# A chunked scan beside two projections: the diagonal part with 64-column sums of squares moved apart from the off-diagonal and state's part

## The chip, the cores and the metric

The kernel runs on one core of a Trainium2 chip. The metric is the device time of one execution in microseconds. The core's engines work side by side and wait for each other by semaphores: PE (TensorE) does matrix products, DVE (VectorE), ACT (ScalarE) and POOL (GpSimd) do elementwise work, SP issues DMAs. Each engine takes its own instructions in the order in which the kernel wrote them.

## What is computed

The reference is a trunk of two layers on a sequence of 1024 tokens of width 1024, in float32. Layer 0 is a spatial gating mixer; layer 1, which the change touches, is a Mamba-2 SSD mixer with 32 heads of 64 channels in 8 groups and a state of 128:

```python
def ssd_mixer(h, w_in, conv_w, conv_b, dt_bias, a_log, d_skip, norm_w, w_out):
    proj = h @ w_in
    z = proj[..., :D_INNER]
    xbc = jax.nn.silu(causal_depthwise_conv(xbc, conv_w, conv_b))
    ...
    w_ls = (cb[..., None] * decay * dt[:, :, None])
    y_diag = jnp.einsum('bclsgj,bcsgjp->bclgjp', w_ls, x)
    states = jnp.einsum('bclgn,bclgj,bclgjp->bcgjpn', Bm, decay_to_end * dt, x)
    _, prev = lax.scan(step, init, (states, chunk_decay))
    y_off = jnp.einsum('bclgn,bcgjpn,bclgj->bclgjp', Cm, prev, jnp.exp(dA_cs))
    y = y_diag + y_off + x * d_skip
    gated = (y * jax.nn.silu(z)).reshape(bsz, L, B_GROUPS, D_INNER // B_GROUPS)
    gated = rmsnorm(gated, norm_w)
    return gated @ w_out
```

Within each chunk of 128 tokens every token sees the earlier ones of its chunk directly (the diagonal part), and all before the chunk through a state that is carried from chunk to chunk (the off-diagonal part). The group norm at the end needs, for each token, the sum of the squares of a group's 256 channels.

## The kernel before

The last third of the kernel is the scan. Its main loop (`scans`) goes over 8 groups x 8 chunks; n = 8·group + chunk counts them. Beside the scan PE works through projections that are still due (`fill`: those of four groups, later the output product), so that it always has something to do. The order on every engine is written out by hand: the loop calls one small function after the other, and `project(upto)` lets the projections catch up to a mark that `want` works out. One step of a projection is six matmuls of 512 columns.

Each chunk calls, on PE:

- `pe_b(n)`: four diagonal matmuls into the tile `yy` (L1626; heads in pairs, 64 columns of the array each, so that two of them lie side by side), two off-diagonal matmuls into the other half of `yy` (L1630, they read the state of chunk n-1), one matmul that makes the state's input `sp` (L1637). In every fourth chunk, with `ends`, two or four matmuls with a column of ones follow, which sum the squares of half a sequence of an earlier group into the other half of `sp` (`sum_b`, L1702), and ACT copies two rows of the result out (L1706). In float32 each of these matmuls is two instructions on PE.
- `project(want(n + .5))`, the first half chunk of projections.
- `pe_a(n + 2)`: three transposes and the B-C product of the chunk after next into `tp` (L1593, L1594).
- `project(want(n + 1))`, the second half.

Behind `pe_a`, and in this order, DVE does `weights(n+1)` (L1617: the decay times the B-C product, which the next diagonal reads), `update(n)` (L1656: state from `sp`), `out(n)` (L1668: off-diagonal part times decay; L1671: both parts and the skip together), one operation of `drain()`, as a rule a tap of the convolution on a finished accumulator `ab` of the projections (L1322), then `tokens(n+2)` (L1607, L1609, from `tp`). ACT makes the decays (L1599, L1601), copies from `tp` (L1611), squares (L1689), casts weights for the projections (L111) and applies silu (L1433, L1423). POOL adds the two output parts (L1674), carries the state (L1647), scales tokens (L1612), gates (L1678), adds the squares' two halves ahead of the sums (L1696) and splits weights (L112).

`yy`, `sp`, `tp` and `pr` (the sums after the scan) share four PSUM tiles of one bank each; an engine that touches a tile waits for the one that used the same bank before. Projections have two accumulators `ab`: the one after next takes over the first one's tile once its last tap is done.

Of the kernel before, what the change touches and what calls it, by code (L numbers as in the profile page):

```python
# [22 lines left out]
G = 8  # L23
# [6 lines left out]
def kernel(  # L30
# [21 lines left out]
    nc = tc.nc  # L52
    x = x[0]
    out = out[0]
# [42 lines left out]
    def sm(name):  # L97
        return ps[0].tile([P, 512], F32, name=name, tag="sm", bufs=n_sm[0])
# [65 lines left out]
    ones = cst.tile([P, P], F32, name="ones")  # L164
# [1146 lines left out]
    def convolve():  # L1311

        finish()
        if todo:
            late.append(todo.pop(0)())
# [75 lines left out]
    def drain(n=1):  # L1391

        for _ in range(min(n, len(queue))):
            for f in queue.pop(0):
                f()
# [153 lines left out]
    def prefetch(g, th):  # L1549

        st = sts[g]
        if g in xbc_d:
            t = st["xbc", th] = s8([P, 4, 512], "xbc")
            nc.sync.dma_start(out=t, in_=xbc_d[g][:, th])
        ze = st["ze", th] = s8([P, 4, 512], "ze")
        if g < G - 1:
            nc.sync.dma_start(out=ze[:, 0:2], in_=z_d[g][:, :, th * 512:(th + 1) * 512])
        for f in range(2):
            for pt in range(2):
                h = 4 * g + 2 * pt + f  # L1560
                nc.sync.dma_start(out=ze[f * 64:(f + 1) * 64, 2 + pt],
                                  in_=ecs_d[h, th * 512:(th + 1) * 512].partition_broadcast(64))

    class Scan:
# [55 lines left out]
        def pe_b(self, c, ends=None):  # L1620

            w, wl = self.cw[c], self.wl.pop(c)
            yy = sm("yy")
            for j in range(4):
                pt, f = j // 2, j % 2
                nc.tensor.matmul(out=yy[f * 64:(f + 1) * 64, pt * P:(pt + 1) * P], lhsT=w[:, j * 64:(j + 1) * 64],  # L1626
                                 rhs=wl[:, j, :], start=True, stop=True)
            if c > 0:
                for pt in range(2):
                    nc.tensor.matmul(out=yy[:, 256 + pt * P:384 + pt * P],  # L1630
                                     lhsT=self.state[c - 1][:, pt * P:(pt + 1) * P], rhs=self.x(3, c),
                                     start=True, stop=True)
            sp = None
            if c < 7 or ends is not None:
                sp = sm("sp")
            if c < 7:
                nc.tensor.matmul(out=sp[:, 0:256], lhsT=w[:, 512:640], rhs=w[:, 256:512], start=True, stop=True)  # L1637
            if ends is not None:
                ends.sum_b(sp[:, 256:512], 2 if ends.g == G - 1 else 1)
            self.ps[c] = yy, sp  # L1640

        def carry(self, c):

# [54 lines left out]
        def sum_b(self, pr=None, n=1):  # L1698
            pr = sm("pr") if pr is None else pr
            for m in range(n):  # L1700
                for h in range(2):
                    nc.tensor.matmul(out=pr[h * 64:h * 64 + 1, 0:256], lhsT=ones[:, 0:1],  # L1702
                                     rhs=self.sq[:, m, h * 256:(h + 1) * 256], start=m == 0, stop=m == n - 1)
            self.sr = self.sq[:, 1, 0:256]
            for h in range(2):
                nc.scalar.copy(out=self.sr[h * 64:h * 64 + 1], in_=pr[h * 64:h * 64 + 1, 0:256])  # L1706
# [5 lines left out]
    def group_rstd(g, t0, n):  # L1712


        c = n // P
        sv = tiny([P, 8], "sv")[:, 0:c]
        nc.sync.dma_start(out=sv, in_=ss_d[g, t0:t0 + n].rearrange("(p c) -> p c", c=c))
        got = []

        def guess():  # L1720
            nc.vector.tensor_scalar(sv, sv, 1.0 / 256, NORM_EPS, ALU.mult, ALU.add)
            got.append(rsqrt_a(sv, c))

        def tail():
            rv = tiny([P, 8], "rvv")[:, 0:c]
            rsqrt_b(rv, sv, got[0], c)
            got.append(rv)

        def put():
            nc.sync.dma_start(out=rs_d[g, t0:t0 + n].rearrange("(p c) -> p c", c=c), in_=got[1])  # L1730

        return guess, tail, put
# [117 lines left out]
    def scans():  # L1850


        chunks = [(g, c) for g in range(G) for c in range(8)]
        N, M = len(chunks), 50
        scan, rs, ran = {}, {}, [0]
        total = 32 * len(plain)

        def fill():
            yield from pj
            yield from bo.product(1, hook_b)  # L1860

        fl = fill()

        def project(upto):
            while ran[0] < upto:
                next(fl, None)
                ran[0] += 1

        def want(at):
            if at < M:  # L1870
                return AHEAD + (total - AHEAD) * at // M
            return total + min(16 * (at - M) // (N - 5 - M), 16 + 2 * (at - N + 5))

        def at(f, n, *a):
            if 0 <= n < N:
                g, c = chunks[n]
                if g not in scan:
                    scan[g] = Scan(g, nc.gpsimd)
                getattr(scan[g], f)(c, *a)

        prefetch(0, 0)
        project(AHEAD // 2 + 1)
        while todo or late:
            convolve()
        for n in range(2):
            at("load", n)
        drain(1)
        for n in range(2):
            at("decay", n)
        drain(len(queue))  # L1890
        at("pe_a", 0), at("tokens", 0), at("weights", 0)
        drain(len(queue))
        project(AHEAD)
        at("pe_a", 1), at("tokens", 1), at("weights", 1)
        at("load", 2)
        for n, (g, c) in enumerate(chunks):
            if n == M + 3:
                drain(len(queue))
            elif n == N - 9:
                for k in range(2):  # L1900
                    bo.get("a", 0, 0, k)
            elif n == N - 7:
                end["scan"] = scan[G - 1]
                bo.get("b", 0, 0, 0)
            p = g if c >= 4 else g - 1
            at("pe_b", n, scan[p] if c % 4 == 3 and p >= 0 else None)
            project(want(n + .5))
            at("pe_a", n + 2)
            if n > 0:
                at("weights", n + 1)  # L1910
            at("update", n)
            at("out", n)
            at("decay", n + 2)
            at("carry", n + 1)
            drain()
            at("tokens", n + 2)
            at("gate", n)
            if n >= N - 7:
                k = n - N + 7
                if k % 2:  # L1920
                    bo.prep(1, k // 2)
                else:
                    bo.ready(0, 0, k // 2)
            at("load", n + 3)
            th = 0 if c >= 4 else 1
            if p >= 0:
                sc = scan[p]
                if p == G - 1:
                    if c == 5:
                        sc.gate_half(th), sc.squares(th)  # L1930
                elif c % 4 == 0:
                    sc.squares(th)
                elif c % 4 == 1:
                    sc.store(th)
                    sc.sum_a()
            if c % 4 == 0 and n >= 8:
                scan[g - 1].sum_c(1 - th)
            if g > 0:
                if c == 5:
                    rs[g] = group_rstd(g - 1, 0, T)  # L1940
                elif c == 6:
                    rs[g][0]()
                elif c == 7:
                    rs[g][1]()
            if c == 0 and g > 1:
                rs[g - 1][2]()
            if c == 1:
                prefetch(g, 1)
            if c == 5 and g < G - 1:
                prefetch(g + 1, 0)  # L1950
            project(want(n + 1))
        sc = scan[G - 1]
        for k in (0, 1):
            bo.get("a", 0, 1, k)
        bo.get("b", 1, 0, 0)
        sc.sum_c(0), rs[G - 1][2]()
        bo.prep(1, 3)
        sc.gate_half(1), sc.squares(1)
        end["half"] = [group_rstd(G - 1, 0, 512)]
        for k in (0, 1):  # L1960
            bo.get("a", 1, 0, k)
        while ran[0] < total + 31:
            project(ran[0] + 1)
        sc.sum_b(n=2)
        sc.sum_c(1)
        for _ in fl:
            pass
# [22 lines left out]
    with tc.manual_schedule():  # L1990
        scans()
        into_end()
# [28 lines left out]
```

## Time and profile before

| What | us |
|---|---|
| median of 3 runs (lowest, highest) | 1517.45 (1517.34, 1518.26) |
| the profiled execution, its own time | 1520.45 |
| its span from the first to the last instruction | 1518.6 |
| busy in the span: DVE, ACT, POOL | 1052.2, 783.3, 402.8 |
| the scan's 64 chunks, first diagonal to last | 1021.7 to 1355.7 of the span |
| PE busy in those 334.0 us | 330.8 |
| DVE, ACT, POOL busy in them | 244.5, 228.1, 222.7 |

Rows of a timeline read: start in us of the span, duration in us, engine, line, operation, output <- inputs, shape, how many were merged; in brackets the idle time of the engine ahead of it and what ended that. Matmuls overlap, so what counts on PE is the distance between starts. Rows of waits read: total us, times, longest.

### The profile page before, as it was taken

What the parts mean: (1) busy time and instruction counts of PE and PEld (TensorE: products, weight loads), DVE (VectorE), ACT (ScalarE), POOL (GpSimd) and SP (SyncE); (2) the same over time, 40 slices, a digit from 0 to 9 for tenths busy, and PEclk for the clock granted to TensorE, in tenths of its full rate; (3) what the DMA queues carried; (4) which work ended last, traced back from release to release, by engine and by line L of the source; (5) the groups of instructions that cost most, each with busy time, mean ns of one, the idle gap of its engine ahead of it and who ended that gap; (6) DMA issues with size and microseconds to landing.
All of it is one profiled execution on the core that took longest, in us unless ns stands there. A gap on an engine that the chain in (4) does not pass through costs nothing. (4 is left out here: it accounts for less than half of the span.)

```text
span 1518.6 us, 21307 instructions
## 1 busy us (share of the span) xinstructions
PE 1475.8 (97%) x7834; PEld 1219.9 (80%) x7834; DVE 1052.2 (69%) x1713; ACT 783.3 (52%) x1256; POOL 402.8 (27%) x451
## 2 busy tenths in 40 slices
PE   6899999999999999999999999989999999999997
PEld 6899988888888888877878788877777777777875
DVE  7956566676666655678656467867677777688876
ACT  6433332322322445556566556656676666756463
POOL 1111110000000023202131323117677666643121
PEclk9999999999999999999999999999999999999999
DMA  5554323332322999947377978787656564679973
GB/s 183 140 173 140 105 89 111 108 107 98 116 86 79 357 255 241 250 140 159 104 178 159 189 162 165 149 231 203 187 165 170 160 191 137 171 248 277 257 149 111
DMA packets 174952, 254.45 MB, mean 168 GB/s; under 512 B 16400, under 2 KB 103168, under 8 KB 171648
## 3 DMA queue, kind: packets, MB, share of 16 engines
q1 hardware_dynamic: 124768, 168.93, 36.6%
q0 software_dynamic: 42448, 70.27, 23.0%
q10 hardware_dynamic: 7632, 13.90, 2.6%
q8 instruction: 62, 1.02, 0.3%
q14 instruction: 42, 0.34, 0.1%
HBM read 186.14 MB, written 51.18 MB: 156 GB/s over the span
## 5 line engine op out<-in xcount | busy, mean ns | idle before, releaser
L134 PE MATMUL acc<-hh,wh 128*128 128x512 f32 x868 | 339.9, 392 | 1.7 <-ACT u L296 1.4
L136 PE MATMUL acc<-hh,wl 128*128 128x512 f32 x868 | 338.5, 390 | 2.0 <-DVE wl L112 1.8
L135 PE MATMUL acc<-hl,wh 128*128 128x512 f32 x868 | 337.8, 389 | 0.0
L112 DVE TENSOR_TENSOR wl<-wr,wh 128x1024 fp32r<-128x1024 f32 (+1 forms) x96 | 114.3, 1192 | 119.4 <-ACT wh L111 119.3
L136 PEld LDWEIGHTS acc<-hh,wl 128*128 128x128 f32 x868 | 162.9, 188 | 37.8 <-DVE wl L112 3.7
L134 PEld LDWEIGHTS acc<-hh,wh 128*128 128x128 f32 x868 | 163.1, 188 | 36.1 <-ACT u L296 2.3
L135 PEld LDWEIGHTS acc<-hl,wh 128*128 128x128 f32 x868 | 163.0, 188 | 33.1
L296 ACT COPY u<-acc 128x512 f32<-128x512 f32 x115 | 66.9, 583 | 197.7 <-PE acc L136 197.6
L111 ACT CAST wh<-wr 128x1024 fp32r<-128x1024 f32 (+1 forms) x112 | 115.2, 1029 | 95.4 <-PE acc L135 56.7
L136 PE MATMUL acc<-wh,hl 128*128 128x256 f32 x448 | 128.6, 287 | 4.8 <-DVE hl L407 3.4
L134 PE MATMUL acc<-wh,hh 128*128 128x256 f32 x448 | 129.2, 288 | 3.0 <-ACT hh L398 1.1
L134 PE MATMUL ab<-hh,wh 128*128 128x512 f32 x288 | 128.2, 445 | 2.8 <-DVE zt L999 1.7
L135 PE MATMUL acc<-wl,hh 128*128 128x256 f32 x448 | 128.1, 286 | 1.1 <-DVE wl L421 1.1
L136 PE MATMUL ab<-hh,wl 128*128 128x512 f32 x288 | 113.4, 394 | 0.0
L135 PE MATMUL ab<-hl,wh 128*128 128x512 f32 x288 | 112.5, 390 | 0.1
L136 PEld LDWEIGHTS acc<-wh,hl 128*128 128x128 f32 x448 | 87.1, 194 | 5.9 <-DVE hl L407 4.1
L134 PEld LDWEIGHTS acc<-wh,hh 128*128 128x128 f32 x448 | 87.3, 195 | 3.9 <-ACT hh L398 1.3
L135 PEld LDWEIGHTS acc<-wl,hh 128*128 128x128 f32 x448 | 87.2, 195 | 1.6 <-DVE wl L421 1.4
L1599 ACT ACTIVATE wl<-wl,tk 128x128 f32<-128x128 f32 x256 | 81.6, 391 | 2.2 <-DMA wl<-cs_d 1.9
L649 POOL DMA_DIRECT2D y_d<-y x8 | 4.4, 549 | 291.3 <-DVE y L646 291.3
L135 PE MATMUL bo<-wl,xh 128*128 128x512 f32 x192 | 76.2, 397 | 3.5 <-DVE wl L742 1.8
L112 DVE TENSOR_TENSOR wl<-t,wh 128x1024 fp32r<-128x1024 f32 (+1 forms) x38 | 45.5, 1196 | 48.5 <-ACT wh L111 48.4
(317 smaller groups left out, 3255.1 us busy)
## 6 DMA issues: line engine op xcount, KB each, us to landing
wr<-in_a_w_in_dram SPq DMA_DIRECT2D x48, 512.0 KB, 3.7
wl<-cs_d SPq DMA_DIRECT2D x64, 256.0 KB, 3.4
wr<-in_b_w_in_dram SPq DMA_DIRECT2D x30, 512.0 KB, 9.1
wb<-in_a_w_out_dram SPq DMA_DIRECT2D x10, 1024.0 KB, 11.8
wb<-in_b_w_out_dram SPq DMA_DIRECT2D x10, 1024.0 KB, 11.1
wr<-in_b_w_in_dram SPq DMA_DIRECT2D x36, 256.0 KB, 8.0
v<-v_d SPq DMA_DIRECT2D x8, 1024.0 KB, 4.8
y_d<-y POOLq DMA_DIRECT2D x8, 1024.0 KB, 5.8
```

Of the source, the lines that this page charges most:

```text
L111: nc.scalar.copy(out=hi, in_=src)
L112: return (eng or nc.vector).tensor_tensor(out=lo, in0=src, in1=hi.bitcast(F32), op=ALU.subtract)
L134: nc.tensor.matmul(out=o, lhsT=l[0], rhs=r[0], start=start, stop=False, **kw)
L135: nc.tensor.matmul(out=o, lhsT=l[0], rhs=r[1], start=False, stop=False, **kw)
L136: nc.tensor.matmul(out=o, lhsT=l[1], rhs=r[0], start=False, stop=stop, **kw)
L296: nc.scalar.copy(out=self.u[n][:, i], in_=a)
L649: store = lambda: nc.gpsimd.dma_start(out=y_d[-1], in_=y)
L1599: nc.scalar.activation(wl[:, j, :], wl[:, j, :], AF.Relu, scale=-1.0, bias=tokc(2, c, self.g)[:, j:j + 1])
```

## The change

`pe_b` keeps the diagonal matmuls and the sums alone. The off-diagonal matmuls and the state's input become a function of their own, `pe_c`, which is called behind the first half of the projections and ahead of the transposes of `pe_a`. `sp` is still allotted in `pe_b`. The sums now use 64 columns of ones and fill 64 rows for each half instead of one; ACT still copies one row of each.

```diff
             yy = sm("yy")
+            sp = None
+            if c < 7 or ends is not None:
+                sp = sm("sp")
             for j in range(4):
...
+            if ends is not None:
+                ends.sum_b(sp[:, 256:512], 2 if ends.g == G - 1 else 1)
+            self.ps[c] = yy, sp
+
+        def pe_c(self, c):
+            w, (yy, sp) = self.cw[c], self.ps[c]
             if c > 0:
                 for pt in range(2):
                     nc.tensor.matmul(out=yy[:, 256 + pt * P:384 + pt * P],
                                      lhsT=self.state[c - 1][:, pt * P:(pt + 1) * P], rhs=self.x(3, c),
                                      start=True, stop=True)
-            sp = None
-            if c < 7 or ends is not None:
-                sp = sm("sp")
             if c < 7:
                 nc.tensor.matmul(out=sp[:, 0:256], lhsT=w[:, 512:640], rhs=w[:, 256:512], start=True, stop=True)
-            if ends is not None:
-                ends.sum_b(sp[:, 256:512], 2 if ends.g == G - 1 else 1)
-            self.ps[c] = yy, sp
...
-                    nc.tensor.matmul(out=pr[h * 64:h * 64 + 1, 0:256], lhsT=ones[:, 0:1],
+                    nc.tensor.matmul(out=pr[h * 64:h * 64 + 64, 0:256], lhsT=ones[:, 0:64],
...
             project(want(n + .5))
+            at("pe_c", n)
             at("pe_a", n + 2)
```

On PE, in a chunk without sums (group 1, chunk 1), the order before was this, with the semaphores that a matmul waits for (PE's names for tiles: `yy`, `sp`, `ab`, `tp` as above):

```order
L1626 MATMUL yy<-wl,cw 64x128 [waits DMAHW3_49,DVE_49,Activation_49]
L1626 MATMUL yy<-wl,cw 64x128 x3
L1630 MATMUL yy<-xbc,state 128x128 [waits DVE_49]
L1630 MATMUL yy<-xbc,state 128x128
L1637 MATMUL sp<-cw 128x256 [waits Pool_49]
L134 MATMUL ab<-hh,wh 128x512
```

The same place in the changed program:

```order
L1629 MATMUL yy<-wl,cw 64x128 [waits DMAHW3_49,DVE_49,Activation_49]
L1629 MATMUL yy<-wl,cw 64x128 x3
L134 MATMUL ab<-hh,wh 128x512
L135 MATMUL ab<-hl,wh 128x512
L136 MATMUL ab<-hh,wl 128x512
L134 MATMUL ab<-hh,wh 128x512
L135 MATMUL ab<-hl,wh 128x512
L136 MATMUL ab<-hh,wl 128x512
L1639 MATMUL yy<-xbc,state 128x128 [waits DVE_49]
L1639 MATMUL yy<-xbc,state 128x128
L1643 MATMUL sp<-cw 128x256 [waits Pool_49]
```

Six projection matmuls have come between the diagonal part and the off-diagonal and state's part.

On PE, in a chunk with sums (group 1, chunk 3, n = 11), one piece of the difference:

```order
-L1626 MATMUL yy<-wl,cw 64x128 [waits DMAHW3_49,DVE_49,Activation_49]
-L1626 MATMUL yy<-wl,cw 64x128 x3
-L1630 MATMUL yy<-xbc,state 128x128 [waits DVE_49]
-L1630 MATMUL yy<-xbc,state 128x128
-L1637 MATMUL sp<-cw 128x256 [waits Pool_49]
-L1702 MATMUL sp<-gsq,ones 1x256 [waits Pool_49]
-L1702 MATMUL sp<-gsq,ones 1x256
+L1629 MATMUL yy<-wl,cw 64x128 [waits DMAHW3_49,DVE_49,Activation_49]
+L1629 MATMUL yy<-wl,cw 64x128 x3
+L1705 MATMUL sp<-gsq,ones 64x256 [waits DVE_49,Pool_49]
+L1705 MATMUL sp<-gsq,ones 64x256
 L134 MATMUL ab<-hh,wh 128x512 [waits DVE_49]
```

and the piece that follows it, half a chunk later:

```order
 L136 MATMUL ab<-hh,wl 128x512
+L1639 MATMUL yy<-xbc,state 128x128 x2
+L1643 MATMUL sp<-cw 128x256 [waits Activation_49]
 L1593 MATMUL tp<-ident,xbc 128x128 [waits PE_49]
 L1593 MATMUL tp<-ident,xbc 128x128 x2
```

The sums stand directly behind the diagonal part and wait for DVE as well as for POOL; the state's input stands behind the sums in the same tile and waits for ACT.

On DVE the order is the same in both programs. Around one chunk it reads, with the changed program's line numbers (L1659, L1671 and L1674 are L1656, L1668 and L1671 of before):

```order
L1617 TENSOR_TENSOR wl<-wl,cw 128x512 [waits DMAHW3_49,DVE_49,Activation_49]
L1659 TENSOR_TENSOR state<-sp,state 128x256 [waits PE_49,Pool_49]
L1671 TENSOR_TENSOR t_8910<-yy,ze 128x256
L1674 SCALAR_TENSOR_TENSOR cw<-xbc,dsk,yy 128x128 x2
L1322 SCALAR_TENSOR_TENSOR bc<-ab,par,bc 128x1021
L1607 TENSOR_TENSOR cw<-tp,tk 128x256 [waits DMAHW4_49,PE_49]
```

Nothing moved here; the state update, the output, the tap and the tokens stand behind each other, and the first of them waits for `sp` from PE.

## The prediction

> **What bounds the kernel now.** I began with the page's table of busy time, then the waits of PE within the scan (1017 to 1380 us of the span), then PE's timeline around single chunks, then the DVE, ACT and POOL rows that feed those chunks. Chunks are numbered n = 8·group + chunk, 0 to 63.
>
> ```profile
> span 1518.6 us, 21307 instructions
> ...
> PE 1475.8 (97%) x7834; PEld 1219.9 (80%) x7834; DVE 1052.2 (69%) x1713; ACT 783.3 (52%) x1256; POOL 402.8 (27%) x451
> ```
>
> The next two rows are the longest waits of PE's matmuls in the scan (total, times, longest).
>
> ```profile
> PE ab L134 <- DVE x L1322: 1.1, 2, 0.7
> PE yy L1626 <- DVE wl L1617: 0.7, 1, 0.7
> ```
>
> PE is the bound, and in the scan it waits for almost nothing. So the change can win only by making PE's own work shorter, and anything that now arrives just in time for PE can cost. The timeline of PE shows a chunk without sums (n = 18) and the next, with sums (n = 19):
>
> ```profile
> 1117.09 0.40 PE L136 MATMUL ab<-hh,wl 128*128 128x512 f32 x1
> 1117.42 0.66 PE L1626 MATMUL yy<-wl,cw 128*64 128x128 f32 x8
> 1118.01 0.71 PE L1630 MATMUL yy<-bc,state 128*128 128x128 f32 x4
> 1118.55 0.60 PE L1637 MATMUL sp<-cw 128*128 128x256 f32 x2
> ...
> 1119.22 0.39 PE L135 MATMUL ab<-hl,wh 128*128 128x512 f32 x1
> ...
> 1120.38 0.38 PE L1593 MATMUL tp<-ident,x 128*128 128x128 f32 x2
> 1120.59 0.27 PE L1593 MATMUL tp<-ident,bc 128*128 128x128 f32 x1
> ...
> 1122.08 0.39 PE L136 MATMUL ab<-hh,wl 128*128 128x512 f32 x1
> 1122.39 0.66 PE L1626 MATMUL yy<-wl,cw 128*64 128x128 f32 x8
> ...
> 1124.06 0.60 PE L1702 MATMUL sp<-gsq,ones 128*1 128x256 f32 x4
> 1124.59 0.50 PE L134 MATMUL ab<-hh,wh 128*128 128x512 f32 x1
> 1124.92 0.39 PE L135 MATMUL ab<-hl,wh 128*128 128x512 f32 x1
> ```
>
> From the last projection matmul ahead of the block to the second behind it: 1119.22 - 1117.09 = 2.13 us without sums, 1124.92 - 1122.08 = 2.84 with them. The sums cost 0.71.
>
> **What the sums save.** What they stream is found where eight of them stand together, after the scan:
>
> ```profile
> 1369.69 1.03 PE L1702 MATMUL pr<-gsq,ones 128*1 128x256 f32 x8
> L1702 PE MATMUL sp<-gsq,ones x64: 377/377/379, 1058.8 to 1357.5; 128*1 128x256 f32 x64
> ```
>
> Eight take 1.03 and four 0.60 (the 1124.06 row), so four more cost 0.43. The other 0.28 of the 0.71 is paid for going from the full array to a narrow one and back. Ahead of the change the sums pay this on their own; behind it they stand next to the diagonal matmuls, which have 64 columns too, and share that group's entry and exit. The 64 sum matmuls of the scan stand at 15 places (14 with four, one with eight): 15 x 0.28 = 4.2 us. Two of them (n = 59 and 63) lie in the tail, which I count apart, so **13 x 0.28 = -3.6**.
>
> Loading 64 columns of ones instead of one is the unknown here. The loads' own rows (min/median/max ns):
>
> ```profile
> L1702 PEld LDWEIGHTS sp<-gsq,ones x64: 79/82/84, 1058.8 to 1357.3; 128*1 128x1 f32 x64
> L1626 PEld LDWEIGHTS yy<-wl,cw x512: 132/137/137, 1021.7 to 1355.9; 128*64 128x64 f32 x171
> ```
>
> 55 ns more per load, four loads, 15 places: 3.3 us if all of it were exposed, 0 if hidden. The diagonal's eight take 0.66 us, four pairs with two such loads each, at most 0.17 a pair, while a pair of sums streams for 0.21. So the loads fit beneath the streaming: I take 0. The Trainium skill, page "TensorE: Matmul & The Clock Gate", section "LDWEIGHTS (loading the stationary operand)", speaks against the change: a load's time goes by its columns, P / 1.2 ns, so an estimate from it is 53 ns for 64 columns against 1 for one, and -4.2 would become -1.0 with all exposed; no row here shows such an exposure.
>
> **What the split costs on PE itself.** In the chunks without sums, the diagonal group's exit now goes into a projection instead of the state's part. Leaving costs 0.10 in the first gap and 0.10 in the second in both rows I have: the state's four matmuls take 1118.55 - 1118.01 = 0.54 where two transposes take 0.21 in steady flow (0.42 for four), and the projection behind the sums has 1124.92 - 1124.59 = 0.33 instead of 0.23. The state's part ahead of the transposes is full array on both sides. Net 0; were the two exits 0.01 apart, ±0.5 over the scan.
>
> **What is late next.** The state's input (sp) and the off-diagonal part come six projection matmuls later, 6 x 0.23 = 1.38 us. DVE runs in order: state update, off-diagonal product, output, one convolution tap, tokens. All of these move 1.38 later against PE.
>
> ```profile
> 1112.43 0.66 PE L1626 MATMUL yy<-wl,cw 128*64 128x128 f32 x8
> 1114.27 0.43 DVE L1656 TENSOR_TENSOR state<-sp,state 128x256 f32<-128x256 f32 x1 [1.37 <-PE sp L1637]
> 1115.45 1.27 DVE L1322 SCALAR_TENSOR_TENSOR x<-ab,par,x 128x1021 f32<-128x1021 f32 x1
> 1117.34 0.27 ACT L1611 COPY cw<-tp 128x128 f32<-128x128 f32 x1 [2.35 <-DVE cw L1609]
> 1126.03 0.73 ACT L1706 COPY gsq<-sp 1x256 f32<-1x256 f32 x2
> ```
>
> In most chunks this costs nothing: the update starts 1114.27 - 1112.43 = 1.84 behind the diagonal, after 1.37 idle, and the weights it ends in have over 2 us until the diagonal that reads them. It costs where a consumer on PE is close behind:
>
> *Accumulators.* A projection starting a new accumulator needs the last tap on the old one.
>
> ```profile
> 1195.23 1.27 DVE L1322 SCALAR_TENSOR_TENSOR x<-ab,par,x 128x1021 f32<-128x1021 f32 x1
> 1196.56 0.50 PE L134 MATMUL ab<-hh,wh 128*128 128x512 f32 x1 [0.44 <-DVE x L1322]
> 1232.86 0.42 DVE L1668 TENSOR_TENSOR t<-yy,ze 128x256 f32<-128x256 f32 x1 [0.39 <-PE yy L1630]
> 1233.72 1.28 DVE L1322 SCALAR_TENSOR_TENSOR bc<-ab,par,bc 128x1021 f32<-128x1021 f32 x1
> 1235.25 0.48 PE L134 MATMUL ab<-hh,wh 128*128 128x512 f32 x1
> 1274.50 0.50 PE L134 MATMUL ab<-hh,wh 128*128 128x512 f32 x1 [0.68 <-DVE x L1322]
> ```
>
> At n = 32 PE starts 0.06 behind the tap's end (1195.23 + 1.27), and the 1274.50 row has the same releaser at n = 46: each loses 1.4. At n = 39, a chunk with sums, the product moves by 1.38 + 0.43 = 1.8; the tap then ends at 1236.8 where PE would be ready at 1235.25 - 0.28: 1.9. Three more accumulators start right behind a diagonal group, 0.6 into the chunk; the tap that ended 0.70 ahead of it (1115.45 + 1.27 against 1117.42 shows the distance) ends 0.7 into it: 3 x 0.17. **+5.2.**
>
> *The sums' bank.* The state's part now comes behind the sums in the same PSUM tile, and the rows of the program's order (section on the change) show it waiting for ACT. The rows of n = 11 show that this wait is for the copies of the sums:
>
> ```profile
> 1081.07 0.74 ACT L1706 COPY gsq<-sp 1x256 f32<-1x256 f32 x2 [2.18 <-PE sp L1702]
> 1081.89 0.42 DVE L1656 TENSOR_TENSOR state<-sp,state 128x256 f32<-128x256 f32 x1 [2.31 <-ACT gsq L1706]
> ```
>
> Before, DVE waited for them; now PE does. Usually ACT is idle and done in time. At n = 19 it isn't: ACT works without a gap from the copy at 1117.34, which waits for DVE's tokens, to the sums' copies, which end at 1126.76. The whole chain moves by 1.38 to 1128.1, and sp's place on PE is 1122.39 + 2.95 = 1125.3: **+2.7** (0.1 taken off for the wait at n = 18). At n = 27 the same chain makes the weights late:
>
> ```profile
> 1163.55 1.68 DVE L1617 TENSOR_TENSOR wl<-wl,cw 128x512 f32<-128x512 f32 x1 [1.31 <-ACT wl L1601]
> 1165.58 0.66 PE L1626 MATMUL yy<-wl,cw 128*64 128x128 f32 x8
> 1168.38 0.73 ACT L1706 COPY gsq<-sp 1x256 f32<-1x256 f32 x2
> ```
>
> They end 0.35 ahead of the diagonal; 1.38 later, PE loses 1.0. Then the copies end at 1169.11 + 1.38 = 1170.5 against 1166.6 + 2.95: another 1.0. **+2.0.**
>
> *POOL.* The sums themselves move 0.7 to 1.2 us ahead, to 0.49 into the chunk, and need POOL's addition.
>
> ```profile
> 1101.16 1.27 POOL L1696 TENSOR_TENSOR gsq<-gsq 128x512 f32<-128x512 f32 x1
> 1101.24 0.66 PE L1626 MATMUL yy<-wl,cw 128*64 128x128 f32 x8
> 1296.73 0.60 PE L1702 MATMUL sp<-gsq,ones 128*1 128x256 f32 x4 [0.50 <-POOL gsq L1696]
> ```
>
> At n = 15 the addition ends at 1102.43, the sums would start at 1101.73: 0.7. At n = 51 POOL sets the time; the off-diagonal and state's part (4 x 0.11 + 0.43 = 0.9), so far done ahead of the sums while POOL was busy, come after them, and the 0.28 won at n = 47 and at n = 51 are lost: 1.5. **+2.2.** In return PE's wait for L1617 at n = 13 (0.5 net) goes, since ACT is through with the sums' copies 0.8 earlier at n = 11: **-0.5.**
>
> *Tail.* At n = 59 sp waits 1.5 for the copies, but PE's slack here hides it:
>
> ```profile
> 1379.79 0.50 PE L135 MATMUL bo<-wl,xh 128*128 128x512 f32 x1 [1.78 <-DVE wl L742]
> ```
>
> DVE and ACT set the time up to there, and their chain shifts by about **+0.4**.
>
> Sum: -3.6 + 5.2 + 2.7 + 2.0 + 2.2 - 0.5 + 0.4 = **+8.4 us**. The profiled execution (1520.45 us, its span 1518.6 and 1.85 around it) would take 1528.9; the same difference on the median of 1517.45 gives **1525.8**.
>
> **Rivals.**
> 1. *Faster.* The waits don't come, because DVE, ACT and POOL make up the shift where they have slack (DVE is busy 69% of the span), and only the switching is left: 1517.45 - 4.2 = 1513.2. For it: PE waits only a few times today. Against it: the rows above show consumers 0.06 to 0.35 us behind their producers. It decides if the waits add up to less than 4. Chance 0.17.
> 2. *No change.* The accumulators' 5.2 come, the chains through ACT and POOL are made up: 1517.45 - 4.2 - 0.5 + 5.2 = 1518. Chance 0.15.
> 3. *The change doesn't do what it says.* The 64-column sums still pay a switch of their own, or expose their loads: 3.3 to 3.6 more than forecast, 1529. Only the argument on pairs speaks against it. Chance 0.10.
> 4. *Forecast*, slower by the waits: 0.58.
>
> About 0.2% (3.0 us) is what a measurement of this kernel can tell from no change. Slower by more has the forecast and the third rival, 0.68; within it 0.15; faster 0.17. The range runs from 1514.5 (below it most of the first rival, some 0.12) to 1531 (the third rival with the exits' 0.5 and some 2 us of waits I haven't found).
>
> **What would show it.** Right: with sums, the block of diagonals and sums takes 2.84 - 0.28 - 0.88 = 1.7 us between the same two projections; DVE's update starts 3.2 us behind the diagonal in a chunk such as n = 17, not 1.84; PE waiting for L1322 at n = 32, 39 and 46 for 2 us each; sp waiting for ACT at n = 19 for over 2 us. Wrong: PE's waits in the scan stay near 3 us in total, or ACT's copies at n = 19 end at their old distance from the diagonal.

## The result and the profile after

| What | before | after |
|---|---|---|
| median (lowest, highest), us | 1517.39 (1515.94, 1518.26) | 1529.38 (1528.81, 1530.85) |
| ratio after/before, 95% interval | | 1.0079 [1.0068, 1.0091] |
| the profiled execution, us | 1520.45 | 1530.85 |
| first to last diagonal matmul of the scan, us | 334.3 | 346.0 |

The kernel is 12.0 us slower. The last line is the cleanest measure: what an execution spends ahead of the scan varies by some us whatever the kernel (the first diagonal starts between 1017.0 and 1021.7 in the nine profiles of this case), and the scan's own length does not contain that. It can be read from one row of each kernel, the first and last start of the diagonal matmuls:

```profile
L1626 PE MATMUL yy<-wl,cw x512: 272/273/323, 1021.7 to 1356.0; 128*64 128x128 f32 x171
```

```profile
L1629 PE MATMUL yy<-wl,cw x512: 272/273/476, 1021.3 to 1367.3; 128*64 128x128 f32 x171
```

The scan alone took 11.6 us more (from starts to the hundredth: 345.96 - 334.33). The longest diagonal matmul is 476 ns instead of 323, which will matter below. The page of the changed kernel and its waits in the scan:

```profile
PE 1475.1 (96%) x7834; PEld 1224.0 (80%) x7834; DVE 1047.1 (68%) x1713; ACT 782.2 (51%) x1256; POOL 404.4 (26%) x451
```

```profile
DVE state L1659 <- PE sp L1643: 60.9, 33, 6.2
...
PE ab L134 <- DVE x L1322: 3.8, 2, 2.1
PE sp L1643 <- ACT gsq L1709: 3.8, 2, 2.5
...
PE ab L134 <- DVE bc L1322: 1.7, 1, 1.7
...
PE sp L1705 <- POOL gsq L1699: 1.1, 2, 0.7
```

PE issues the same 7834 matmuls (1475.1 us busy, 1475.8 before) and now waits for DVE, ACT and POOL. DVE in turn waits 60.9 us for `sp`, 25.5 before:

```profile
DVE state L1656 <- PE sp L1637: 25.5, 20, 2.6
```

Each stands still for the other in turn.

The timeline of PE and DVE at a chunk without sums (n = 17):

```profile
1111.25 0.39 PE L136 MATMUL ab<-hh,wl 128*128 128x512 f32 x1
1111.57 0.66 PE L1629 MATMUL yy<-wl,cw 128*64 128x128 f32 x8
...
1112.50 0.40 PE L135 MATMUL ab<-hl,wh 128*128 128x512 f32 x1
...
1114.81 0.42 DVE L1659 TENSOR_TENSOR state<-sp,state 128x256 f32<-128x256 f32 x1 [2.46 <-PE sp L1643]
```

DVE's update starts 1114.81 - 1111.57 = 3.24 behind the diagonal. And at the next chunk with sums (n = 19), with the ACT row that PE waits for:

```profile
1121.42 0.39 PE L136 MATMUL ab<-hh,wl 128*128 128x512 f32 x1
1121.73 0.66 PE L1629 MATMUL yy<-wl,cw 128*64 128x128 f32 x8
1122.22 0.60 PE L1705 MATMUL sp<-gsq,ones 128*64 128x256 f32 x4
...
1123.09 0.39 PE L135 MATMUL ab<-hl,wh 128*128 128x512 f32 x1
...
1124.24 0.61 PE L1639 MATMUL yy<-bc,state 128*128 128x128 f32 x4
1126.58 0.73 ACT L1709 COPY gsq<-sp 1x256 f32<-1x256 f32 x2
1127.36 0.70 PE L1643 MATMUL sp<-cw 128*128 128x256 f32 x2 [2.51 <-ACT gsq L1709]
...
1129.16 0.63 PE L136 MATMUL ab<-hh,wl 128*128 128x512 f32 x1
1129.59 0.63 PE L134 MATMUL ab<-hh,wh 128*128 128x512 f32 x1
```

Diagonals and sums take 1123.09 - 1121.42 = 1.67 between the projections. `sp` comes 2.7 late, when ACT's copies end (1126.58 + 0.73). The last two rows are the unforeseen part: 1.3 us after the wait the projections stand 0.43 apart, not 0.23. The view by windows shows the granted clock of PE (the column before the last two) in the window of 3.4 us that holds a long wait, and in the next one:

```profile
core 0: us, PE busy (x) PEld busy (x) DVE busy (x) ACT busy (x) POOL busy (x), PEclk, DMA share, GB/s
1125.20:1128.60 3.40, 1.24 (x8) 1.14 (x9) 1.19 (x4) 3.35 (x9) 1.24 (x2) 1.00 0.02 5
1128.60:1132.00 3.40, 3.40 (x15) 2.08 (x13) 3.31 (x7) 1.39 (x4) 2.26 (x4) 0.50 0.02 5
1200.30:1203.70 3.40, 1.62 (x10) 1.25 (x8) 3.31 (x8) 0.85 (x3) 1.44 (x3) 1.00 0.75 185
1203.70:1207.10 3.40, 3.40 (x15) 2.12 (x14) 0.34 (x1) 3.37 (x4) 2.71 (x2) 0.50 0.91 312
1241.20:1244.60 3.40, 1.73 (x13) 1.45 (x12) 2.57 (x7) 1.83 (x5) 2.92 (x4) 1.00 0.13 43
1244.60:1248.00 3.40, 3.40 (x21) 2.47 (x20) 3.30 (x6) 3.19 (x4) 3.27 (x3) 1.00 0.08 14
1282.20:1285.60 3.40, 1.35 (x6) 1.05 (x6) 3.39 (x8) 0.79 (x2) 1.72 (x3) 1.00 0.00 0
1285.60:1289.00 3.40, 3.40 (x17) 2.08 (x16) 0.22 (x1) 3.37 (x3) 3.40 (x3) 0.50 0.13 46
```

Behind the waits at n = 19, 32 and 46 PE runs at half its clock for one such window; behind that at n = 39 it doesn't. Compared with the same distances at full clock, the three cost 1.5, 1.5 and 1.6: 4.6 us.

The rows of the waits at n = 32, 39 and 46 answer to those shown of before:

```profile
1202.52 0.50 PE L134 MATMUL ab<-hh,wh 128*128 128x512 f32 x1 [1.78 <-DVE x L1322]
...
1242.89 1.28 DVE L1322 SCALAR_TENSOR_TENSOR bc<-ab,par,bc 128x1021 f32<-128x1021 f32 x1
1244.22 0.50 PE L134 MATMUL ab<-hh,wh 128*128 128x512 f32 x1 [1.67 <-DVE bc L1322]
...
1284.25 0.50 PE L134 MATMUL ab<-hh,wh 128*128 128x512 f32 x1 [2.07 <-DVE x L1322]
```

Where the 11.6 us arise, from the start of each chunk's diagonal, counted from that of n = 0, after minus before:

| n | 19 | 21 | 26 | 28 | 32 | 34 | 39 | 40 | 46 | 48 | 59 | 63 |
|---|---|---|---|---|---|---|---|---|---|---|---|---|
| us | -0.3 | 3.8 | 3.5 | 5.3 | 5.0 | 7.9 | 7.8 | 9.4 | 8.7 | 11.4 | 11.2 | 11.6 |

Between the five steps the line falls by 0.3 at each chunk with sums: that is the gain. The steps are the waits at n = 19, 26 and 27, 32, 39 and 46, three of them with a window at half clock behind.

### The profile page after: what moved, and what is told of

It reads as the page before. It is cut to its first block, busy times and chain, and to the rows that moved or that the text cites. A ratio compares the mean times of both kernels' runs of the same rounds, so it can differ in the third digit from the quotient of the medians.

```text
span 1528.7 us, 21318 instructions
## 1 busy us (share of the span) xinstructions
PE 1475.1 (96%) x7834; PEld 1224.0 (80%) x7834; DVE 1047.1 (68%) x1713; ACT 782.2 (51%) x1256; POOL 404.4 (26%) x451
## 5 line engine op out<-in xcount | busy, mean ns | idle before, releaser
L134 PE MATMUL acc<-hh,wh 128*128 128x512 f32 x868 | 339.8, 392 | 1.3 <-ACT u L296 1.3
L134 PEld LDWEIGHTS ab<-hh,wh 128*128 128x128 f32 x288 | 54.7, 190 | 29.1 <-issue 12.1
```

The source lines that it names most:

```text
L134: nc.tensor.matmul(out=o, lhsT=l[0], rhs=r[0], start=start, stop=False, **kw)
```

## The experiments

Beside each time stands the scan's length from the profiled execution (before 334.3, after 346.0). The kernel before took 1516.85 us beside four of these runs (the width alone, the unsplit block with 64 columns, the sums behind the state's input, three taps first) and 1516.69 beside the other three. First come the runs on what the sums save, then those on the waits.

**The width alone.** The kernel before, with 64 columns of ones and nothing moved.

```diff
-                    nc.tensor.matmul(out=pr[h * 64:h * 64 + 1, 0:256], lhsT=ones[:, 0:1],
+                    nc.tensor.matmul(out=pr[h * 64:h * 64 + 64, 0:256], lhsT=ones[:, 0:64],
```

> The kernel before with one edit: the sums have 64 columns of ones instead of one, at their old place behind the full-array matmuls. My theory: nothing is won, since the sums still go from the full array to a narrow one and back on their own, and nothing is lost, since the loads fit beneath the streaming: 1517.4 us, within 1 of before. Rival, that loading 64 columns is exposed: 3.3 us slower, 1520.7. Rival, that the width itself is the gain: 4.2 faster, 1513.2.

Measured: 1517.45 us, ratio 1.0002 [0.9993, 1.0010], scan 334.6. The width by itself neither wins nor costs what a time can show. The timeline of PE at n = 19 of this kernel does show a little:

```profile
1124.17 0.65 PE L1702 MATMUL sp<-gsq,ones 128*64 128x256 f32 x4
```

The four sums take 0.65 instead of 0.60, and the distances between diagonals grow by 0.05 to 0.06 at the places of the sums: 0.8 us at 15 places at most. That fits one load of four that shows when the sums stand behind a full-array matmul (the prediction's rows have 55 ns more per load), but no run separates it. The scan is only 0.3 longer because a DMA wait of 0.4 at n = 42 is missing here. Behind the diagonal they took 0.60 (the 1122.22 row of the changed kernel): there the loads are hidden, as the prediction had it.

**The changed kernel with narrow sums.**

```diff
-                    nc.tensor.matmul(out=pr[h * 64:h * 64 + 64, 0:256], lhsT=ones[:, 0:64],
+                    nc.tensor.matmul(out=pr[h * 64:h * 64 + 1, 0:256], lhsT=ones[:, 0:1],
```

> The changed kernel with one column of ones and one output row for each sum, as in the kernel before; everything else as changed. Theory (the sums save their switch of 0.28 us only because they have the 64 columns of the diagonal matmuls): the switch is paid again at 13 places of the scan, 13 x 0.28 = +3.6, of which some is hidden where sums wait for POOL: 1531 to 1533 us, and four sums stand 0.2 to 0.3 us longer behind the diagonal. Rival (sums behind the diagonal part are cheap whatever their width, one change from narrow to another narrow shape costs nothing): 1529.4, no difference from the changed kernel.

Measured: 1528.59 us, ratio 1.0071 [1.0059, 1.0083], scan 345.2. The theory failed by its number: there is no loss of 2 to 4 us. PE at n = 19 of this kernel:

```profile
1120.00 0.39 PE L136 MATMUL ab<-hh,wl 128*128 128x512 f32 x1
1120.32 0.66 PE L1629 MATMUL yy<-wl,cw 128*64 128x128 f32 x8
1120.90 0.60 PE L1705 MATMUL sp<-gsq,ones 128*1 128x256 f32 x4
...
1121.77 0.40 PE L135 MATMUL ab<-hl,wh 128*128 128x512 f32 x1
```

The block takes 1.77, against 1.67 with 64 columns. The sums start 0.58 behind the first diagonal instead of 0.49, and the way out is equal (0.87 from the sums to the second projection in both). So the width is worth 0.10 of the 0.28 at each place, and the neighbourhood of the diagonal the other 0.18. The 13 x 0.10 = 1.3 are lost in this run's time behind the clock: its 2.7 us wait at n = 19 fell into two windows and was followed by no half clock, one such stretch fewer than in the changed kernel's profile.

**One unsplit block**, ordered so that the diagonal and the 64-column sums come last; the kernel before otherwise.

```diff
...
             if c < 7:
                 nc.tensor.matmul(out=sp[:, 0:256], lhsT=w[:, 512:640], rhs=w[:, 256:512], start=True, stop=True)
+            if c > 0:
+                for pt in range(2):
...
+            for j in range(4):
+                pt, f = j // 2, j % 2
...
             if ends is not None:
                 ends.sum_b(sp[:, 256:512], 2 if ends.g == G - 1 else 1)
```

> The kernel before with the block in another order and not split: state's input, off-diagonal part, diagonal part, sums with 64 columns, then the projections. The sums share the diagonal's narrow stretch, nothing that DVE waits for comes later, and the sums come as late as before. My theory: the 0.28 at 13 to 15 places is won and no wait is added: 1517.4 - 3.6 to 4.2 = 1513.5 us. Rival, that the switch isn't saved beside the diagonal: 1517.4. Rival, that the state's part, now the first of the block, waits for the state of the chunk ahead: slower than before by 1 or more.

Measured: 1513.02 us, ratio 0.9973 [0.9962, 0.9984], scan 331.1. **This beats both kernels.** It has the sums' gain without moving `sp` behind the first half of the projections, and no wait of 2 us in the scan. The same with one column of ones:

```diff
-                    nc.tensor.matmul(out=pr[h * 64:h * 64 + 64, 0:256], lhsT=ones[:, 0:64],
+                    nc.tensor.matmul(out=pr[h * 64:h * 64 + 1, 0:256], lhsT=ones[:, 0:1],
```

> The one block of the experiment before (state's input, off-diagonal, diagonal, sums; unsplit) with one column of ones for each sum. Theory: the width is worth 13 to 15 switches of 0.28, so 1513.0 + 3.6 to 4.2 = 1516.6 to 1517.2, as the kernel before. Rival (the order alone wins, the width nothing): 1513.0.

Measured: 1514.16 us, ratio 0.9984 [0.9976, 0.9993], scan 332.0. It lies between both expectations: of 3.8 us the order brings 2.5 and the width 1.1 to 1.3 by the medians. The two intervals overlap, so as a time the width's share isn't shown; the scans differ by 0.9, and the rows show where. The rows of PE, first with 64 columns, then with one:

```profile
1118.97 0.66 PE L1636 MATMUL yy<-wl,cw 128*64 128x128 f32 x8
1119.46 0.60 PE L1702 MATMUL sp<-gsq,ones 128*64 128x256 f32 x4
```

```profile
1120.18 0.66 PE L1636 MATMUL yy<-wl,cw 128*64 128x128 f32 x8
1120.77 0.60 PE L1702 MATMUL sp<-gsq,ones 128*1 128x256 f32 x4
```

0.49 against 0.59 from diagonal to sums: the price of 0.10 again, paid where the shape changes.

**The sums behind the state's input.** The changed kernel, with the sums moved from the diagonal to the end of `pe_c`. That takes away both waits that the sums' new place made (`sp` behind ACT's copies, the sums early for POOL) and keeps the late `sp`.

```diff
-            if ends is not None:
-                ends.sum_b(sp[:, 256:512], 2 if ends.g == G - 1 else 1)
...
-        def pe_c(self, c):
+        def pe_c(self, c, ends=None):
...
+            if ends is not None:
+                ends.sum_b(sp[:, 256:512], 2 if ends.g == G - 1 else 1)
...
-            at("pe_c", n)
+            at("pe_c", n, scan[p] if c % 4 == 3 and p >= 0 else None)
```

> The changed kernel with the sums moved back behind the state's input, half a chunk later, still 64 columns wide. My theory: PE's waits for ACT's copies at n = 19 and 27 (2.8 and 1.0 us) and for POOL at n = 15 and 51 (0.6 and 0.8) go, the slow-clock stretch behind the wait at n = 19 (1.8) goes, and the sums pay 0.28 again at 13 places (3.6): 1529.4 - 8.0 + 3.6 = 1525.0 us. The accumulators' waits at n = 32, 39, 46 stay. Rival, that the moved sums cost nothing and the split of the block by itself is what costs: 3.6 to 4.2 slower than the changed kernel, 1533.

Measured: 1524.46 us (1520.24 to 1524.77), ratio 1.0044 [1.0031, 1.0058], scan 339.8. The time is near the 1525.0 expected (with 1.8 for the stretch at half clock behind n = 19, which measures 1.5), and the rival's 1533 is out. The waits for ACT's copies and for POOL are gone; those for the tap stay:

```profile
PE ab L134 <- DVE x L1322: 3.7, 2, 2.1
...
PE ab L134 <- DVE bc L1322: 1.7, 2, 0.9
```

The profiled execution is the one of 1520.24, and it is instructive. It has the waits at n = 32 and 46 (1.9 and 2.3 from start to start), and no half clock behind them (columns as above):

```profile
1271.50:1274.90 3.40, 1.98 (x14) 1.60 (x12) 1.86 (x5) 0.00 (x0) 0.74 (x2) 1.00 0.26 74
1274.90:1278.30 3.40, 2.75 (x17) 1.95 (x18) 2.22 (x5) 2.17 (x3) 2.60 (x4) 1.00 0.00 0
```

The wait at n = 46 is cut by a window's border and leaves PE 1.98 and 2.75 us busy in the two. The other four executions took 1523.7 to 1524.8 and have no profile. Half clock behind their waits may be why: their mean granted clock was 0.993 to 0.996, against 0.997 here. But so may the stretch ahead of the scan, which took 1017.0 us here and 1018.4 to 1021.7 in the other eight profiles. The record doesn't separate the two.

**Three taps first.** The changed kernel with the tap called ahead of the state update on DVE in the chunks n = 32, 39 and 46.

```diff
+            if n in (32, 39, 46):
+                drain()
             at("update", n)
             at("out", n)
             at("decay", n + 2)
             at("carry", n + 1)
-            drain()
+            if n not in (32, 39, 46):
+                drain()
```

> The changed kernel with DVE's order altered in three chunks, n = 32, 39 and 46: the convolution's tap stands ahead of the state update and the output instead of behind them. My theory: PE's waits for the tap there fall by 4.6 us to at most before's or none (all together 6.2 now), and with them the stretches of half clock that follow n = 32 and 46 (3.0): 1529.4 - 6.2 - 3.0 = 1520.2 us, at least 1521.8. Rival, that the accumulators' waits are made up for later (another wait takes their place): within 2 us of the changed kernel. Rival on the clock: the half-clock stretches come from something else than the waits and stay: 1523.2.

Measured: 1524.09 us, ratio 1.0039 [1.0026, 1.0052], scan 340.9. The waits at n = 39 and 46 vanish, that at n = 32 shrinks from 2.0 to 1.2, and the half clock behind n = 32 and 46 goes with them: 1.8 (n = 39) + 2.3 (n = 46) + 0.85 (n = 32) + 3.1 (the clock) = 8.0 us saved. The scan wins only 5.0, because new waits come at n = 35 (`sp` for the copies, 0.8) and n = 49 (the weights, 0.8), and the one at n = 51 grows from 0.8 to 2.3:

```profile
1298.16 0.66 PE L1629 MATMUL yy<-wl,cw 128*64 128x128 f32 x8
1300.99 0.44 PE L1705 MATMUL sp<-gsq,ones 128*64 128x256 f32 x2 [2.17 <-POOL gsq L1699]
```

A wait on PE gives the other engines time to catch up. Taken away, it comes back at the next place where PE is close behind.

**The block with two taps first.** The one block with 64 columns, and the tap first at n = 32 and 46.

```diff
+            if n in (32, 46):
+                drain()
             at("update", n)
...
-            drain()
+            if n not in (32, 46):
+                drain()
```

> The one block of the experiment before, with 64 columns, and the convolution tap of the chunks n = 32 and n = 46 called ahead of the state update on DVE. In its profile PE waits 0.68 us at n = 32 and 0.34 us at n = 46 for that tap. Theory: both waits go, 1.0 us less: 1512.0. Rival (as with three taps in the changed kernel, the update and the product of these chunks then come later, and other waits take their place): 1513.0 or above.

Measured: 1512.54 us, ratio 0.9967 [0.9955, 0.9979], scan 330.4. Both waits are gone from the trace, the one at n = 51 (`sp` for POOL) grew from 0.8 to 1.0, and the scan is 0.8 shorter. The interval overlaps that of the block without it, so as a time the difference isn't shown.

## Why it came out as forecast, and which terms were off

The predicted change was +8.4 us, the measured one +12.0 in the medians; the forecast's mechanism (PE waits because all of DVE's chain is later) is what happened. Its signs are all there: the block of 1.7 us (1.67), the update 3.2 us behind the diagonal (3.24), the three waits for L1322 of some 2 us each, `sp` over 2 us late at n = 19. Term by term, from the profiled execution (distances of starts on PE against the usual ones):

| Term | forecast | measured |
|---|---|---|
| sums beside the diagonal | -3.6 | -3.7 |
| split on PE itself | 0 | 0 |
| accumulators | +5.2 | +5.2 |
| sums' bank, n = 19 | +2.7 | +2.8 |
| n = 26 and 27 | +2.0 | +2.1 |
| POOL, n = 15 and 51 | +2.2 | +1.0 |
| wait ahead of n = 13 gone | -0.5 | -0.5 |
| a DMA wait at n = 42 gone | not seen | -0.4 |
| half clock behind three waits | not priced | +4.6 |
| n = 59 to the tail's wait for L742 | +0.4 | +0.45 |

The row of n = 42 need not be the change's doing: that wait is missing from the trace of the width alone too. The sum of the right column is 11.55; the matmul behind the wait for L742 comes 11.65 later than before, counted from the first diagonal. Behind it before has one window at half clock and after none, which gives 0.9 back.

- **Sums.** Measured at n = 19 as 2.84 - 0.88 - 1.67 = 0.29; 13 places with 0.28 to 0.30 each make 3.7. The size was right and the reason only in part. The prediction let the sums share the diagonal's entry and exit because both have 64 columns. The two runs with narrow sums show that standing next to each other brings 0.18 of the 0.28 at any width, and equal shape 0.10.
- **Split on PE.** At n = 17 the diagonal's block takes 1112.50 - 1111.25 = 1.25, and the off-diagonal and state's part put ahead of the transposes 0.87 (1119.71 - 1118.84 in the rows below); together 2.12 against 2.13 unsplit.

```profile
1118.84 0.60 PE L1639 MATMUL yy<-bc,state 128*128 128x128 f32 x4
...
1119.71 0.38 PE L1593 MATMUL tp<-ident,x 128*128 128x128 f32 x2
```

- **Loads of 64 columns.** Taken as 0, and 0 behind the diagonal. By the estimate from the Trainium skill's page "TensorE: Matmul & The Clock Gate", section "LDWEIGHTS (loading the stationary operand)", 3.2 us were at stake; no row of the changed kernel shows them.
- **Accumulators, the sums' bank, n = 26 and 27.** Right to 0.1. Each was worked out from the distance between a consumer on PE and the end of its producer's chain.
- **POOL.** Mis-sized: at n = 51 PE waits 0.8, only 0.3 more than before, where 1.5 was forecast. The forecast shifted this place by the change's own parts and left out that PE comes there later because of n = 46 (1.4 us more of waiting and 1.6 of half clock), which gives POOL time. With the n = 46 wait taken away (the three taps) the wait is 2.3.

```profile
1306.83 0.65 PE L1705 MATMUL sp<-gsq,ones 128*64 128x256 f32 x4 [0.67 <-POOL gsq L1699]
```

- **The clock.** The missing term and the largest: it more than fills the gap between forecast and result. The prediction took each wait at its own length. The profile of before had the hint, in the tail:

```profile
1377.40:1380.80 3.40, 1.62 (x7) 1.05 (x6) 3.40 (x5) 2.48 (x2) 1.34 (x1) 1.00 0.98 333
1380.80:1384.20 3.40, 3.40 (x9) 2.64 (x8) 3.40 (x5) 3.09 (x4) 0.00 (x0) 0.51 0.98 189
```

The 1.78 us wait for L742 quoted in the prediction is followed by 3.4 us at half clock.

That the time still lies inside the range is in part luck: the range went up to 1531 for the third rival and for some 2 us of waits not found, and what filled that room was the clock, less 1.2 us that POOL was priced too high.

Of the rivals, the third named almost the measured time, 1529, but for a reason that isn't there: the sums pay no switch of their own. The first and second fall, since the waits sum to 11.1 us without the clock (5.2 + 2.8 + 2.1 + 1.0), and DVE, ACT and POOL made up little of the shift at these places, although DVE is idle for 32% of the span.

## What to carry to other kernels

A part of a chain that crosses engines isn't moved for nothing because the engine it runs on does the same work: work out, for each consumer, how close it stands behind its producer, and shift the chain. Gain a neighbour by changing the order within a block before splitting the block: the same 64-column sums win 3.8 us where the state's input stays early and lose 12.0 where it goes half a chunk later. And where a wait on PE passes some 1.8 us, price the half-clock window that may follow it: some 1.5 us more here.

## What was unexpected of the hardware

**A wait of 2 us can be followed by 3.41 us at half clock.** In the changed kernel's trace the windows at half clock start at 1128.6, 1203.7 and 1285.6. Their distances are 75.1 and 81.9 us, 22 and 24 times 3.41: they lie on a grid. In the scan and its tail, what tells the windows ahead of half clock from the others is PE's busy time in one window of that grid. In the profiles of five kernels, windows with 0.89, 1.24, 1.35, 1.37, 1.48, 1.62 and 1.62 us busy were followed by half clock, and those with 1.65, 1.70, 1.72, 1.73, 1.93, 1.98 and 2.10 by full clock. The pair nearest to the border is that at n = 32 of the changed kernel (1.62, half) and the tail's wait with three taps first:

```profile
1382.40:1385.80 3.40, 1.65 (x8) 1.05 (x7) 3.40 (x5) 2.48 (x2) 1.34 (x1) 1.00 0.94 324
1385.80:1389.20 3.40, 3.40 (x17) 2.80 (x16) 3.19 (x5) 3.09 (x4) 0.00 (x0) 1.00 1.00 170
```

So a wait of the same length costs some 1.5 us more or nothing, by where the grid's border falls in that execution. At n = 19 the wait of 2.7 us was followed by half clock in the changed kernel and not with narrow sums, where it lay across a border:

```profile
1121.60:1125.00 3.40, 1.93 (x10) 1.48 (x10) 1.81 (x3) 3.37 (x7) 2.59 (x5) 1.00 0.30 98
1125.00:1128.40 3.40, 2.45 (x13) 1.93 (x13) 2.34 (x6) 2.79 (x9) 0.32 (x2) 1.00 0.02 5
```

The Trainium skill, page "TensorE: Matmul & The Clock Gate", section "What's actually happening", describes a free-running window of 3413 ns and a clock that is either full or half; the traces agree with both. It gives an idle window of about 3.4 us as the condition for half clock; here a window that PE was busy in for up to 1.62 of its 3.41 us was enough. That the busy share is the true condition was read from these windows, not tested by a kernel made for it. Outside the scan it doesn't hold everywhere: in the one block's profile the window from 40.6 us (1.69 us busy) is followed by half clock, and at the kernel's end those from 1507.1 us before (1.60) and from 1507.0 us with the sums behind the state's input (1.50) are followed by full clock. So the border near 1.6 us is a reading of the scan and its tail alone, and the condition itself stays open.
